# Mixture-of-experts stage: pairs of experts in two 64-column tiles replaced by quads in four 32-column tiles with wide passes of 128 slots

## Chip, cores and metric

One core of a Trainium2 chip runs the whole program: two transformer blocks over 512 tokens of width 1024, in fp32. The metric is the device time of one execution in microseconds (us), of which the median of several runs is given. The change touches one stage only, the hierarchical mixture of experts (MoE) of the first block.

## What is computed

The stage is this part of the reference, with 512 tokens, 4 groups of 8 experts, the best group and its two best experts for each token, and an expert width of 256:

```python
def hierarchical_moe(h, w_group, b_group, w_router, b_router, w_gate, w_up, w_down):
    t = h.reshape(-1, d)
    group_prob = jax.nn.softmax((t @ w_group + b_group), axis=-1)
    p_group, g_idx = lax.top_k(group_prob, 1)
    expert_logits = (t @ w_router + b_router).reshape(-1, N_GROUPS, EXPERTS_PER_GROUP)
    in_group = jnp.einsum('tg,tge->te', one_hot(g_idx[:, 0]), expert_logits)
    w_top, e_idx = lax.top_k(jax.nn.softmax(in_group, axis=-1), TOP_K)
    w_top = w_top / jnp.sum(w_top, axis=-1, keepdims=True) * p_group
    expert_ids = g_idx * EXPERTS_PER_GROUP + e_idx
    combine = jnp.sum(one_hot(expert_ids, N_EXPERTS) * w_top[..., None], axis=1)
    for e in range(N_EXPERTS):
        hid = jax.nn.silu(t @ w_gate[e]) * (t @ w_up[e])
        out = out + combine[:, e:e + 1] * (hid @ w_down[e])
    return out
...
    x = x + gate2[:, None, :] * ffn
```

Both kernels compute an expert only for the tokens that chose it. How many these are is known only during the run, so the number of passes is decided by branches.

## The kernel before

`Net.moe` begins by writing the normalised tokens to device memory (`h2d`) and working out, with comparisons and two matmuls, the `rank` of each token within each expert. An expert's tokens are then taken in slots: `select` (L1170 to L1178) compares ranks with a row of slot numbers (`iota`), and four small matmuls (L1174) turn the one-hot matrix into token numbers, weights and output rows. `gather` (L1193) fetches the tokens of the slots from `h2d` by an indirect DMA.

The 32 experts go through in 16 pairs, in the order of the list `order`. A pair is two neighbours of one group; each has 64 slots, and the two stand side by side in two 64-column tiles of the TensorE array. For a pair:

- `xpose` (L1214) transposes the gathered tokens by eight matmuls with the identity, and `feed` (L1202 on ScalarE, L1204 on VectorE) scales them into the tiles `xgT`.
- `expert1` (L1245) runs the gate and up projections: 8 slices of the depth, each for both experts, with 512 columns of weights; tanh (L1250) and two VectorE operations (L1251, L1252) make the hidden tile `mth`.
- `turn` (L1258) transposes the hidden tile by two matmuls, with an eviction on ScalarE (L1260).
- `expert2` (L1279) runs the down projection, ScalarE scales it by the weights (L1280), and GpSimd scatters the rows to `yd` by an indirect DMA (L1284). The last two pairs are added by matmuls instead (`combine`, L1293).

The loop over `n` places the gate/up of pair n ahead of the down of pair n - 1, so that the hidden tile of a pair is made and turned beside other matmuls.

When an expert of the pair has more than 64 tokens, `more` (L1318) runs a further pass of 64 slots, and a second one above 128 (L1324). `ahead` (L1305, L1307) gathers their tokens one pair early. The further passes are called through `again`; their tiles are `oxg`, `cy`, `th` and `rsb`. Passes beyond the third are all in `rest`, under one branch (L1379) that is taken when any expert has over 192 tokens. `count` (L1301) loads the larger count of a pair into a register of every engine.

The weights of an expert come in three tiles of 1 MiB, two for gate/up and one for down (`load`, L1026), all issued by SyncE from a pool of 12 tiles, which is two pairs. `load(n + 2)` stands behind the branches of pair n. At the end `fetch` (L1337) reads `yd` back in four transfers, each with both rows of 128 tokens; `collect` adds them on GpSimd (L1343), transposes them (L1347) and adds them to the residual (L1351).

A scheduler sets the order of each engine's instructions, and it may move one past a whole branch.

Of the kernel before, what the change touches and what calls it, by code (L numbers as in the profile page):

```python
# [46 lines left out]
def layout(a):  # L47
# [35 lines left out]
    gu = gu.reshape(NE, KT, P, 512).transpose(0, 2, 1, 3).reshape(NE, P, 4096)  # L83
# [45 lines left out]
def constants():  # L129
# [37 lines left out]
    o["iota"] = np.ascontiguousarray(np.broadcast_to(1 + np.arange(512).reshape(8, 64), (P, 8, 64)).astype(f))  # L167
# [36 lines left out]
class Net:  # L204
# [804 lines left out]
    def moe(self):  # L1009
        nc, v, s, g_, pe = self.nc, self.nc.vector, self.nc.scalar, self.nc.gpsimd, self.nc.tensor  # L1010
        A, tc, mp = self.A, self.tc, self.mp
        mm, ident, ones, mod = pe.matmul, self.ident, self.ones, self.mod

        wt = {}

        order = [4 * g + i for i in range(4) for g in range(4)]
        NP = NE // 2

        NL = 2

        def load(n, part=(0, 1)):

            for o in (0, 2048) * (0 in part) + (4096,) * (1 in part):
                for e in (2 * order[n], 2 * order[n] + 1):
                    w = wt[e, o] = self.t(self.mw, [P, 2048], "wmoe")
                    nc.sync.dma_start(w, A["wmoe"][e, :, o:o + 2048])  # L1026

        u128 = self.const("u128", [P, P], pool=mp)
        iota = self.const("iota", [P, 8, 64], pool=mp)
        tokens = iota.rearrange("p a b -> p (a b)")  # L1030
        prio = self.const("prio", [P, 8], pool=mp)
        tokb = self.const("tokb", [P, 4], pool=mp)
        load(0, (0,))
        load(1, (0,))
# [4 lines left out]
        xgs = [self.t(mp, [P, D], f"xg{q}") for q in range(3)]  # L1039
        oxg = [self.t(mp, [P, D], f"oxg{q}") for q in range(4)]  # L1040
        for t in xgs + oxg:
            g_.memset(t, 0.0)
# [3 lines left out]
        xn = [self.t(mp, [P, D], "htok", bufs=4) for _ in range(4)]  # L1046
        for i in range(4):
# [5 lines left out]
            nc.sync.dma_start(h2d[i * P:(i + 1) * P, :], xn[i])  # L1053
        load(0, (1,))
        load(1, (1,))
# [53 lines left out]
        cnt = sm([1, NE], "cnt")  # L1109
        v.tensor_copy(cnt, psr[0:1, 4, :])  # L1110
        cm = sm([1, 17], "cm")
        v.tensor_max(cm[:, 0:16], cnt[:, 0::2], cnt[:, 1::2])
        v.tensor_reduce(cm[:, 16:17], cm[:, 0:16], axis=AX.X, op=ALU.max)
        cmi = self.t(mp, [1, 17], "r_cmi32", I32)
        v.tensor_copy(cmi, cm)
# [22 lines left out]
        val = sm([P, 4, NP, 5], "val")  # L1138
# [11 lines left out]
        def oindex(p, r):  # L1150

            t = opair[p if r == 1 else NP + p % 4 if r == 2 else NP + 4]
            return (t if p >= NP - NL else t.bitcast(U32))[:, 0:1], t.bitcast(U32)[:, 1:2]

# [741 lines left out]
```

## Time and profile before

| what | value |
| --- | --- |
| median of 3 runs | 2215.34 us (2214.61 to 2220.91) |
| the profiled execution | 2215.8 us |
| its span, first to last instruction | 2214.0 us |
| TensorE (PE) busy, whole span | 2072.9 us, 94% |
| instructions, whole span | 32214 |
| MoE stage: its first weights issued | 447.55 us |
| first gate/up matmul | 493.41 us |
| last product into the residual ends | 855.32 us |
| weight tiles of the stage | 96 of 1024 KB, 11.7 us from issue to landing |

The span lies 1.8 us below the time of the same execution, and that time 0.5 us above the median. The share of TensorE over the whole span hides the stage: the blocks around it keep the engine busy all the time, while inside it the share changes from stretch to stretch. So the stage is read by stretches of its own, and then pair by pair. In the trace's names PE is the matmul engine, PEld its weight loads, DVE is VectorE, ACT ScalarE, POOL GpSimd and SP SyncE; a name with q behind it (PEldq) is the engine's instruction queue, where branches and register loads stand. One fp32 matmul of the code stands as two records.

### The profile page before, as it was taken

To read this page: it belongs to the slowest core of one execution; us is meant where nothing else is said; L and a number is where in the kernel's file an instruction comes from. 1 tells how busy PE (TensorE), PEld (TensorE's weight loads), DVE (VectorE), ACT (ScalarE), POOL (GpSimd) and SP (SyncE) were. 2 spreads that over 40 slices of the span, in tenths; PEclk is the share of its full clock that TensorE was granted. 3 is DMA by queue.
4 is the path that set the end of the run, shared out by engine and by line. 5 is a ranking of instruction groups with operands and counts; after the bars stand their busy time and mean duration, and the time that the engine had idled before them with its cause. 6 is when DMAs were issued, how large, how long until landed. Compare 5 with 4: busy or idle time off the path is not lost. (4 is left out here: it accounts for less than half of the span.)

```text
span 2214.0 us, 32214 instructions
## 1 busy us (share of the span) xinstructions
PE 2072.9 (94%) x12908; PEld 1569.1 (71%) x12908; DVE 1075.8 (49%) x2071; ACT 718.0 (32%) x1197; POOL 203.4 (9%) x223
## 2 busy tenths in 40 slices
PE   5999999788888978999999899999999999999996
PEld 3677767553433427888888888888878888888886
DVE  4663665642222217653253855746574447542444
ACT  3432442121222223322232434525352244322221
POOL 3020002010111113000001400000000032000002
PEclk9999999798898988999999999999999999999998
DMA  7343215075958972323332322323132322233321
GB/s 263 115 128 112 96 43 178 25 289 208 375 202 346 377 297 100 108 96 92 103 95 86 96 67 93 98 76 115 53 104 96 110 86 77 95 87 103 102 89 39
DMA packets 93877, 294.53 MB, mean 133 GB/s; under 512 B 15746, under 2 KB 27010, under 8 KB 81404
## 3 DMA queue, kind: packets, MB, share of 16 engines
q1 hardware_dynamic: 86364, 278.03, 36.2%
q0 software_dynamic: 7328, 14.01, 1.9%
q8 instruction: 119, 1.95, 0.3%
q14 instruction: 66, 0.54, 0.1%
HBM read 286.12 MB, written 20.23 MB: 138 GB/s over the span
## 5 line engine op out<-in xcount | busy, mean ns | idle before, releaser
L272 PE MATMUL mm<-xh,wh 128*128 128x512 f32 (+1 forms) x1584 | 614.4, 390 | 8.3 <-ACT xh L1510 4.5
L273 PE MATMUL mm<-xl,wh 128*128 128x512 f32 (+1 forms) x1584 | 604.7, 382 | 4.4 <-DVE xl L1511 4.2
L274 PE MATMUL mm<-xh,wl 128*128 128x512 f32 (+1 forms) x1584 | 602.1, 381 | 0.0
L255 ACT ACTIVATE wh<-wraw 128x1024 fp32r<-128x1024 f32 (+3 forms) x282 | 274.2, 974 | 745.7 <-PE mm L273 659.2
L256 DVE TENSOR_TENSOR wl<-wraw,wh 128x1024 fp32r<-128x1024 f32 (+3 forms) x282 | 315.0, 1118 | 192.9 <-ACT wh L255 187.4
L272 PEld LDWEIGHTS mm<-xh,wh 128*128 128x128 f32 x1584 | 301.4, 191 | 74.1 <-issue 8.0
L273 PEld LDWEIGHTS mm<-xl,wh 128*128 128x128 f32 x1584 | 302.4, 191 | 60.7 <-DVE xl L1511 6.2
L274 PEld LDWEIGHTS mm<-xh,wl 128*128 128x128 f32 x1584 | 301.6, 191 | 56.3 <-issue 1.2
L338 POOL TENSOR_TENSOR ss<-ss,sq 128x256 f32<-128x256 f32 (+1 forms) x69 | 67.0, 972 | 929.3 <-ACT sq L337 913.3
L272 PE MATMUL mm<-hh,wh 128*128 128x512 f32 (+1 forms) x416 | 148.5, 357 | 0.0
L274 PE MATMUL mm<-hh,wl 128*128 128x512 f32 (+1 forms) x416 | 148.3, 357 | 0.0
L273 PE MATMUL mm<-hl,wh 128*128 128x512 f32 (+1 forms) x416 | 148.3, 356 | 0.0
L1245 PE MATMUL mm<-wmoe,xgT 128*64 128x512 f32 x512 | 127.6, 655 | 5.9 <-issue 5.8
L1245 PEld LDWEIGHTS mm<-wmoe,xgT 128*64 128x64 f32 x512 | 41.4, 153 | 82.6 <-issue 74.7
L273 PEld LDWEIGHTS mm<-hl,wh 128*128 128x128 f32 x416 | 78.6, 189 | 11.4
L272 PEld LDWEIGHTS mm<-hh,wh 128*128 128x128 f32 x416 | 78.6, 189 | 11.2
L274 PEld LDWEIGHTS mm<-hh,wl 128*128 128x128 f32 x416 | 78.6, 189 | 11.2
L1571 DVE TENSOR_TENSOR sq<-mm,rsb 128x512 f32<-128x512 f32 x44 | 30.4, 691 | 104.0 <-PE mm L274 103.8
L1566 DVE TENSOR_TENSOR cy<-mm,rsb 128x512 f32<-128x512 f32 x44 | 30.4, 690 | 85.5 <-PE mm L274 83.5
L1251 DVE SCALAR_TENSOR_TENSOR mth<-mth,mm 128x256 f32<-128x256 f32 x16 | 6.7, 421 | 113.9 <-ACT mth L1250 113.9
L1279 PE MATMUL mm<-wmoe,hT 128*64 128x512 f32 x256 | 57.8, 592 | 0.0
L1202 ACT ACTIVATE xgT<-mm,mod,gs 128x128 f32<-128x128 f32 x64 | 27.9, 462 | 77.2 <-DVE xgT L1204 64.8
(495 smaller groups left out, 2620.6 us busy)
## 6 DMA issues: line engine op xcount, KB each, us to landing
wmoe<-in_wmoe SPq DMA_DIRECT2D x96, 1024.0 KB, 11.7
wraw<-in_win SPq DMA_DIRECT2D x90, 512.0 KB, 3.5
wraw<-in_wgu SPq DMA_DIRECT2D x88, 512.0 KB, 3.3
wraw<-in_wada SPq DMA_DIRECT2D x32, 512.0 KB, 3.7
wraw<-in_wd SPq DMA_DIRECT2D x32, 448.0 KB, 3.3
big<-in_wada SPq DMA_DIRECT2D x16, 512.0 KB, 6.0
wraw<-in_wd SPq DMA_DIRECT2D x16, 512.0 KB, 3.5
wraw<-in_wout SPq DMA_DIRECT2D x16, 256.0 KB, 2.5
```

The source lines that it names most:

```text
L255: self.nc.scalar.activation(h[:, :n], raw[:, :n], AF.Copy)
L256: self.nc.vector.tensor_sub(l[:, :n], raw[:, :n], h[:, :n])
L272: mm(ps, w1, xh[k], start=start and i == 0, stop=False)
L273: mm(ps, w1, xl[k], start=False, stop=False)
L274: mm(ps, w2, xh[k], start=False, stop=stop and i == nk - 1)
L338: self.nc.gpsimd.tensor_add(acc[:, hs], acc[:, hs], sq[:, hs])
L1202: s.activation(xTs[hf][:, k, :], pt[:, k, :], AF.Identity, scale=self.gs2[:, kk:kk + 1], bias=mod[:, 3, kk:kk + 1])
L1245: mm(pg_[cs, :], xT[k // 4][:, k % 4, cs], piece(p, c, k // 4 * 2048 + k % 4 * S, r), start=k == 0, stop=k == KT - 1)
L1251: v.scalar_tensor_tensor(th, th, 1.0, pg_[:, :256], op0=ALU.add, op1=ALU.mult)
L1279: mm(py[cs, :], hT[:, k, cs], piece(p, c, 4096 + k * 1024 + n * S, r), start=k == 0, stop=k == 1)
L1566: v.tensor_mul(t1, pp[0], rb)
L1571: v.tensor_mul(t2, pp[1], rb)
```

## The change

- Quads: the loop runs over 8 quads. Quad q holds expert q of each of the four groups, each with 32 slots, in four 32-column tiles.
- Wide passes: an expert's tokens beyond the first 32 go through `wide_pass`, with 128 slots of this expert alone on the whole array; up to four such passes are nested in `more`. Gate and up columns are stored in two halves (in `layout`), so that the first half's hidden tile is made beside the second half's matmuls. `gather_wide` gathers for a wide pass, and `ahead` does so for the first pass of each expert, behind the previous quad's passes.
- `rest` and its branch are gone. Down follows gate/up and turn of the same quad; it no longer stands behind the next one's gate/up.
- Weights come in six tiles of 512 KB for an expert, from a pool of 31. `load(31)` stands at the stage's start, and `load(6)` behind the passes of each expert.
- `count` loads six values for each quad (four experts, and the larger of each two), 48 in place of 17.
- The stores of `h2d` go from SyncE's queue to ScalarE's; only the last quad is added by matmuls, in place of two pairs.

The core of the diff (the added `layout` line for the halves, `select`, which does four experts with 32 slots, and the tail are left out):

```diff
+        NQ = NE // 4
+        first, wide = 32, 128
+        def ex(q, c):
+            return 8 * c + q
+        todo = iter([(ex(q, c), j) for q in range(NQ) for js in (range(4), range(4, 6)) for c in range(4) for j in js])
+        def load(n):
+            for e, j in islice(todo, n):
+                w = wt[e, j] = self.t(self.mw, [P, 1024], "wmoe")
+                nc.sync.dma_start(w, A["wmoe"][e, :, 1024 * j:1024 * j + 1024])
+        load(self.nmw)
...
-            nc.sync.dma_start(h2d[i * P:(i + 1) * P, :], xn[i])
+            nc.scalar.dma_start(h2d[i * P:(i + 1) * P, :], xn[i])
...
+        def gather_wide(e, r):
+            lo = first + wide * (r - 1)
+            v.tensor_tensor(oh1, iota[:, lo:lo + wide].unsqueeze(1).to_broadcast([P, 4, wide]),
+                            rank[:, :, e].unsqueeze(2).to_broadcast([P, 4, wide]), ALU.is_equal)
+            pv = self.pst([P, 3], "mm")
+            for i in range(4):
+                mm(pv, oh1[:, i, :], val[:, i, e, :], start=i == 0, stop=i == 3)
...
+            fetch_tokens(oxg[e // 8], u[:, 1:2])
...
+        def expert1(q, xT):
+            ps = self.pst([P, 2, 2, P], "mm")
             for k in range(KT):
+                for c in range(4):
+                    cs = slice(32 * c, 32 * c + 32)
+                    mm(ps[cs].rearrange("p a b c -> p (a b c)"), xT[k // 4][:, k % 4, cs], piece(ex(q, c), k),
+                       start=k == 0, stop=k == KT - 1, tile_position=(0, 32 * c))
+            th = self.t(mp, [P, 2, P], "mth")
+            glu(th, ps[:, :, 0, :], ps[:, :, 1, :])
             return th
...
+        def wide_pass(e, r):
+            xT = xpose(oxg[e // 8], oxT)
+            pt = None
+            for a in range(2):
+                ps = self.pst([P, 2, P], "mm")
+                for k in range(KT):
+                    mm(ps.rearrange("p a b -> p (a b)"), xT[k // 4][:, k % 4, :], piece(e, k)[:, 256 * a:256 * a + 256],
+                       start=k == 0, stop=k == KT - 1)
+                    if a and k == 4:
+                        pt = self.pst([P, P], "mm")
+                        pe.transpose(pt, oth[:, 0, :], ident)
+                        s.copy(ohT[:, 0, :], pt)
+                glu(oth[:, a, :], ps[:, 0, :], ps[:, 1, :])
+            py = [self.pst([P, S], "mm") for _ in range(2)]
+            for k in range(2):
+                if k:
+                    pt = self.pst([P, P], "mm")
+                    pe.transpose(pt, oth[:, 1, :], ident)
+                    s.copy(ohT[:, 1, :], pt)
+                for n in range(2):
+                    mm(py[n], ohT[:, k, :], wt[e, 4 + k][:, n * S:(n + 1) * S], start=k == 0, stop=k == 1)
+            for n in range(2):
+                s.activation(yt[1][:, n * S:(n + 1) * S], py[n], AF.Copy, scale=oix[e, r][:, 2:3])
+            scatter(yt[1], oix[e, r].bitcast(U32)[:, 0:1])
...
+        def ahead(q):
+            for h in range(2):
+                with tc.If(rvs[NE + 8 * h + q] > first):
+                    for c in (2 * h, 2 * h + 1):
+                        with tc.If(rvs[ex(q, c)] > first):
+                            gather_wide(ex(q, c), 1)
+        def more(e, r=1):
+            if r < 5:
+                with tc.If(rvs[e] > first + wide * (r - 1)):
+                    if r > 1:
+                        gather_wide(e, r)
+                    wide_pass(e, r)
+                    more(e, r + 1)
...
+        for q in range(NQ):
+            last = q == NQ - 1
+            th = expert1(q, xt)
+            if q == 0:
+                ahead(0)
+            if not last:
+                xt = xpose(gat[q + 1][0])
+                count(q + 1)
             hT = turn(th)
+            if not last:
+                expert2(q, hT, *gat[q][1:3])
+                if q + 2 < NQ:
+                    gat[q + 2] = gather(q + 2)
+            for c in range(4):
+                more(ex(q, c))
+                load(6)
+            if not last:
+                ahead(q + 1)
+        got = [fetch(i) for i in range(4)]
...
-                self.mw = pool(s1, "mw", 12, reuse_waits="tile")
+                self.nmw = 31
+                self.mw = pool(s1, "mw", self.nmw, reuse_waits="tile")
```

Three places of the program, as its engines receive it. `mm` is an accumulator, `wmoe` a weight tile, `c_ident` the identity, `xg` gathered tokens, `htok` in the changed kernel those of a wide pass, `cy` and `th` (in two tiles) the fed tokens and the hidden tile of a further or wide pass, `rsb` its turned hidden tile, `r_cmi` the counts, `r_val` and `cy` as operands of a small matmul the values and the one-hot matrix.

On TensorE before, where pair 2 follows pair 1, the turn of the pair before stands just ahead of the gate/up matmuls of the pair:

```order
L1214 MATMUL mm_5571<-c_ident_64,xg_725_4670 128x128 x4
L1214 MATMUL mm_5580<-c_ident_64,xg_725_4670 128x128 x4
L1258 MATMUL mm_5589<-c_ident_64,mth_5350 128x128 x2
L1245 MATMUL mm_5594<-wmoe_5296,xgT_899_5569 64x512
L1245 MATMUL mm_5594<-wmoe_5298,xgT_899_5569 64x512
```

On TensorE now, at the end of the first quad's gate/up:

```order
L1255 MATMUL mm_5114<-wmoe_4673,xgT_849_4956 32x512
L1227 MATMUL mm_5207<-c_ident_64,xg_4714 128x128 x4
L1227 MATMUL mm_5216<-c_ident_64,xg_4714 128x128 x4
L1264 MATMUL mm_5309<-c_ident_64,mth_5147 128x128 x2
L1287 MATMUL mm_5314<-wmoe_4675,hT_5312 32x512
```

The turn now belongs to the same quad: it follows its last gate/up matmul with only the eight transposes for the next quad between, and down follows at once.

On TensorE before, behind a further pass, from the end of its branches to the next pair:

```order
L1324 UNCONDITIONAL_BRANCH x2
L1318 UNCONDITIONAL_BRANCH
L1301 TENSOR_LOAD r_cmi_773_4820
L1305 COMPARE_AND_BRANCH
L1174 MATMUL mm_5766<-r_val_4849,cy_4854 128x5 x4
L1307 COMPARE_AND_BRANCH
L1174 MATMUL mm_5784<-r_val_4849,cy_4854 128x5 x4
L1307 UNCONDITIONAL_BRANCH x2
L1305 UNCONDITIONAL_BRANCH x2
L1174 MATMUL mm_5814<-r_val_4849,oh_5809 128x5 x4
```

On TensorE now, the end of an expert's first wide pass, and what is jumped over behind it when there is no second one:

```order
L1316 MATMUL mm_5414<-wmoe_4675,rsb_4926 128x512
L1316 MATMUL mm_5415<-wmoe_4675,rsb_4926 128x512
L1313 MATMUL mm_5418<-c_ident_64,th_4881 128x128
L1316 MATMUL mm_5414<-wmoe_4677,rsb_4926 128x512
L1316 MATMUL mm_5415<-wmoe_4677,rsb_4926 128x512
L1346 COMPARE_AND_BRANCH
L1202 MATMUL mm_5430<-r_val_4874,cy_4878 128x3 x4
L1227 MATMUL mm_5441<-c_ident_64,htok_751_4731 128x128 x4
```

Each expert has four such passes in its place in the code, one inside the other, where a pair had two.

On SyncE before, the loads of a pair stand between the branches of the look-ahead and those of the next pair's passes:

```order
L1305 COMPARE_AND_BRANCH
L1307 COMPARE_AND_BRANCH
L1307 UNCONDITIONAL_BRANCH x2
L1305 UNCONDITIONAL_BRANCH x2
L1026 DMA wmoe_5797<-in_wmoe 128x2048
L1026 DMA wmoe_5799<-in_wmoe 128x2048
L1026 DMA wmoe_5801<-in_wmoe 128x2048
L1026 DMA wmoe_5803<-in_wmoe 128x2048
L1026 DMA wmoe_5805<-in_wmoe 128x2048
L1318 COMPARE_AND_BRANCH
```

On SyncE now, behind the 31 loads of the start, the end of the 48 register loads and the first quad's passes:

```order
L1333 TENSOR_LOAD r_cmi_785_4845
L1333 ISA x2
L1346 COMPARE_AND_BRANCH x4
L1346 UNCONDITIONAL_BRANCH x5
L1031 DMA wmoe_5644<-in_wmoe 128x1024
L1346 COMPARE_AND_BRANCH x4
L1346 UNCONDITIONAL_BRANCH x5
```

All 48 register loads have moved ahead of the 32nd weight load, and that load alone stands behind the first expert's passes; the next 21 follow the branches of the other three experts and of the look-ahead.

## Rows read from the trace of the kernel before

**Rows 1.** Windows: stretch, length; busy us (count) by engine; PEclk; DMA share; GB/s

```profile
493.00:560.00 67.00, 56.21 (x257) 24.64 (x258) 19.58 (x81) 13.46 (x30) 10.51 (x9) 0.86 0.54 201
...
720.00:808.00 88.00, 79.68 (x373) 32.39 (x371) 18.67 (x61) 21.78 (x48) 10.12 (x10) 0.93 0.86 349
```

**Rows 2.** TensorE groups, 490 to 860 us: busy us, mean ns | idle before

```profile
L1245 PE MATMUL mm<-wmoe,xgT 128*64 128x512 f32 x512 | 127.6, 655 | 5.9 <-issue 5.8
L1279 PE MATMUL mm<-wmoe,hT 128*64 128x512 f32 x256 | 57.8, 592 | 0.0
...
L1245 PE MATMUL mm<-wmoe,cy 128*64 128x512 f32 x80 | 18.3, 599 | 0.3
```

**Rows 3.** TensorE timeline: start us, us, operation, count [idle before <-releaser]

```profile
493.41 7.09 PE L1245 MATMUL mm<-wmoe,xgT 128*64 128x512 f32 x32
...
522.68 1.09 PE L1214 MATMUL mm<-c_ident,oxg 128*128 128x128 f32 x8
523.84 3.65 PE L1245 MATMUL mm<-wmoe,cy 128*64 128x512 f32 x16
527.32 3.60 PE L1245 MATMUL mm<-wmoe,th 128*64 128x512 f32 x16
532.41 0.41 PE L1258 MATMUL mm<-c_ident,th 128*128 128x128 f32 x2 [1.48 <-DVEq L1324]
533.33 5.35 PE L1279 MATMUL mm<-wmoe,rsb 128*64 128x512 f32 x16 [0.52 <-ACT rsb L1260]
540.16 1.03 PE L1174 MATMUL mm<-r_val,oh 128*128 128x5 f32 x8 [1.48 <-PEq L1305]
...
543.32 7.65 PE L1245 MATMUL mm<-wmoe,xgT 128*64 128x512 f32 x32
550.81 3.60 PE L1279 MATMUL mm<-wmoe,hT 128*64 128x512 f32 x16
555.58 1.03 PE L1174 MATMUL mm<-r_val,oh 128*128 128x5 f32 x8 [1.17 <-PEq L1305]
```

**Rows 4.** Timeline, stage's end: reads of rows, an addition, last products

```profile
819.54 2.85 SPq L1337 DMA_DIRECT2D wmoe<-yd  x4
...
824.96 2.35 POOL L1343 TENSOR_TENSOR wmoe<-wmoe 128x1024 f32<-128x1024 f32 x1 [15.23 <-DMA wmoe<-yd]
...
851.10 4.22 DVE L1351 SCALAR_TENSOR_TENSOR x<-mm,mod,x 128x128 f32<-128x128 f32 x16
```

**Rows 5.** TensorE timeline at the only 32-column tiles of this kernel

```profile
129.40 0.64 PE L392 MATMUL sm<-wraw,ca 128*32 128x256 f32 x8
129.97 0.70 PE L636 MATMUL mm<-xx,c_ublk 128*128 128x512 f32 x1
```

**Rows 6.** Control by line: duration ns min/median/max, first and last start us

```profile
L1301 SPq TENSOR_LOAD <-r_cmi x16: 263/270/468, 481.4 to 779.8; - x16
...
L1301 PEldq TENSOR_LOAD <-r_cmi x16: 298/302/498, 497.8 to 795.0; - x16
...
L1318 PEldq COMPARE_BRANCH  x16: 70/348/922, 498.4 to 825.7; - x16
...
L1305 PEldq COMPARE_BRANCH  x19: 70/208/1011, 502.1 to 795.4; - x19
...
L1379 PEldq COMPARE_BRANCH  x1: 6410/6410/6410, 809.0 to 809.0; - x1
```

**Rows 7.** TensorE timeline behind the branch at L1379

```profile
817.66 0.66 PE L1258 MATMUL mm<-c_ident,mth 128*128 128x128 f32 x2 [7.98 <-DVEq L1379]
```

**Rows 8.** Windows as in the first group: two stretches of transfers

```profile
575.00:600.00 25.00, 22.02 (x85) 9.63 (x85) 6.93 (x29) 5.54 (x13) 5.10 (x5) 0.73 0.98 392
0.00:15.00 15.00, 0.00 (x0) 0.00 (x0) 4.74 (x9) 5.40 (x9) 7.04 (x13) 1.00 0.69 222
```

**Rows 9.** DMA issues of the page: count, KB each, us to landing

```profile
wraw<-in_wgu SPq DMA_DIRECT2D x88, 512.0 KB, 3.3
```

**Rows 10.** DMA queues of the page: packets, MB, share

```profile
q8 instruction: 119, 1.95, 0.3%
```

More of the change, by code (lines that the diff above doesn't have):

```diff
@@ L1 @@
 import math
-from itertools import chain
+from itertools import chain, islice
 import numpy as np
@@ new lines, in moe @@
+        v.tensor_copy(val[:, :, :, 0], tokb.unsqueeze(2).to_broadcast([P, 4, NE]))
+        v.tensor_copy(val[:, :, :, 1], wa)
+        v.scalar_tensor_tensor(val[:, :, :, 2], a2, float(S), tokb.unsqueeze(2).to_broadcast([P, 4, NE]), op0=ALU.mult, op1=ALU.add)
+        q1, q2, q3, q4 = (self.t(self.tp, [P, S], "cy" if q < 2 else "th") for q in range(4))
+        oix = {(e, 1): self.t(mp, [P, 4], f"oix{e}") for e in range(NE)}
+        for r in range(2, 5):
+            for c in range(4):
+                t = self.t(mp, [P, 4], f"oix_{c}_{r}")
+                oix.update({(ex(q, c), r): t for q in range(NQ)})
@@ L1270, in expert2 @@
+        def expert2(q, hT, idx, wv):
+            late = q == NQ - 1
+            ys = yt[:1]
             if late:
-                ys.append(oC if r else self.t(self.tp, [P, S], "sq", F32R))
+                ys = [self.t(mp, [P, D], f"ys{i}", F32R) for i in range(2)]
+                ys.append(self.t(self.tp, [P, S], "sq", F32R))
                 v.tensor_scalar(ys[-1], tokens, idx, None, op0=ALU.is_equal)
@@ L1294, in combine @@
                 v.scalar_tensor_tensor(self.x[k][:, hs], ps, mod[:, 5, k:k + 1], self.x[k][:, hs], op0=ALU.mult, op1=ALU.add)
-                yield
         rvs = {}
-        full = slice(0, S)
-        def count(p):
-            rvs[p] = nc.values_load(cmi[0:1, order[p]:order[p] + 1], min_val=0, max_val=S)
-        def ahead(p):
-            with tc.If(rvs[p] > 64):
-                gather(p, 1)
-                with tc.If(rvs[p] > 128):
-                    gather(p, 2)
-        def again(p, r, xg):
-            th = expert1(p, xpose(xg, r), r)
-            ys = expert2(p, turn(th, r), oindex(p, r)[0], oweight(p, r), r)
-            if p >= NP - NL:
-                drain(combine(ys, full))
@@ new lines, in ahead @@
+        def ahead(q):
+            for h in range(2):
+                with tc.If(rvs[NE + 8 * h + q] > first):
[9 more added lines that the diff above has]
+                    more(e, r + 1)
@@ L1344, in collect @@
+        def fetch(i):
+            ys = [self.t(self.mw, [P, D], "wmoe") for _ in range(2)]
+            for a in range(2):
+                nc.sync.dma_start(ys[a], yd[a * S + i * P:a * S + (i + 1) * P, :])
+            return ys
+        def collect(i, ys):
+            y = ys[0]
+            g_.tensor_add(y, y, ys[1])
             for hf in range(2):
```

225 lines of the change are left out of this document (71 added, 154 removed).

## The prediction

> **What bounds the kernel now.** I read the stretches of the stage first, then the costliest groups, then one pair's timeline, and last the control flow and the transfers. From 493 to 560 us TensorE is busy for 56.2 of 67 us, with a DMA share of 0.54; from 720 to 808 for 79.7 of 88, with 0.86 [rows 1]. So TensorE sets the end, and the transfers wait for it. Nearly all its time is two groups, the gate/up matmuls (127.6 us in the plain passes) and the down matmuls (57.8 us) [rows 2]. The reader is to see there that a matmul moves 512 columns, whether 2 or 60 of its 64 slots hold tokens.
>
> A plain pair costs 15.4 us, from the selection at 540.16 to that at 555.58; its parts are 8 transposes, the turn, 7.65 us of gate/up (7.09 where the clock was full) and 3.60 us of down. A further pass costs 17.5 us, from its transposes at 522.68 to the next selection at 540.16, since nothing covers it: between its gate/up and its down lie 2.41 us (from 530.92 to 533.33), its down takes 5.35 instead of 3.60 us after that gap, and another 1.48 us pass before TensorE works again [rows 3]. The gate/up of the further passes has 80 records of its first half, 16 a pass [rows 2], so there are five; the inputs say so too (expert loads of group 1: 117, 34, 64, 145, 73, 55, 84, 86; no expert of another group has over 29). So 16 pairs at about 15 us and 5 passes at 17.5 us make some 330 us of the way from 493.4 us, when gate/up begins, to the last addition's end at 855.3 [rows 3, 4].
>
> **What the change does to it, part by part.** On these inputs each quad has one expert over 32 tokens, of group 1, and never over 160: eight plain quads and eight wide passes, one in each quad.
>
> *Quads.* 32 gate/up matmuls on four 32-column tiles. What says that four run at once is the one place of the kernel with such tiles: eight records of 256 columns last 0.64 us, and the next instruction starts 0.57 us after the first [rows 5]. A pair's 32 records of 512 columns last 7.09 us, two at a time; by the same pace eight records of 256 would take 0.89 us two at a time and 0.44 four at a time, so 0.57 fits four with its start. A quad's gate/up then costs 7.0 us and its down 3.6, what a pair cost. The chain in the quad is now serial: gate/up 7.0, transposes for the next quad 1.09 (inside the gap), wait and turn up to 2.41 in all, down 3.6, selection 1.0, a branch and its drain 0.6. With the transposes counted whole, 15.7 us. I take 15.6, since a part of the gap covers them.
>
> *Wide pass.* Transposes and feed 1.16 us (522.68 to 523.84), 16 matmuls of 256 columns on the whole array, 32 records. A 512-column record alone takes 0.427 us (7.09/32 is 0.222 for one of two side by side, so twice that less the start), a 256-column one 0.213; 32 of these 6.8. Then 0.26 for a transpose in their midst, the wait of 2.41 behind the last of them (in part under the first two down matmuls of 1.7 us, which I count in it), and two more down matmuls 1.7: 12.4 us, against the 17.5 us of a 64-slot pass [rows 3]. Eight of them are 99 us, where five passes of before were 87.5. So here the change costs 12 us, while the plain part falls from 16 times 15.4 to 8 times 15.6, by 122 us.
>
> *Control between quads.* After the wide pass TensorE's queue passes two more experts' branches, six register loads at 0.302 us (1.8), and some six branches of the look-ahead at 0.208 median (1.2) [rows 6]. With 0.35 for each of three branches of the passes (1.0), the selection matmuls 1.0 and 0.9 for the one-hot ahead of them (an estimate: the gap of 1.48 less a load and two branches), 5.9 us. All of it is exposed; nothing is queued behind it that could run first. It comes seven times, and 4.9 once at the start. I add 0.6 for a drain and 2.0 a quad for the clock after gaps (5.35 against 3.60 [rows 3]; the granted clock of the two stretches is 0.86 and 0.93 [rows 1]).
>
> *What goes.* The big branch over all the fourth and later passes takes 6.41 us, and TensorE idles 7.98 [rows 6, 7]; that code is now inside each `more`, below.
>
> *Loads.* 192 half-MiB tiles. At 392 GB/s, the rate of a stretch with a share of 0.98, a quad's 24 tiles take 32.1 us; at the rate that the start of the kernel implies for short rows, 222 GB/s at a share of 0.69, so 322, they take 39.1 [rows 8]. I take 32, as that row is this very transfer. 18 of a quad's tiles come free only when its wide pass ends. At that point 13 of the next quad's 24 are in. A tile of this size lands 3.3 us after its issue where nothing queues [rows 9], about 2 more than its 1.34 of transfer, so the last three gate/up tiles are in 6 us later, under the 5.9 us of control and the first matmuls, and all eleven after 16.7, where down begins 0.6 + 5.9 + 7.0 + 1.09 + 2.41 = 17.0 us after. That is hidden, but without slack. The 48 register loads of SP, all ahead of its first wait for a free tile, take 48 x 0.27 = 13 us plus the check of their bounds [rows 6] and lie under the 31 tiles already issued (41 us at 392 GB/s).
>
> *Tail.* From the last wide pass: scatter and landing 6 us, the first read of the rows 3 to 5 (read issued 819.54, first addition 824.96), four additions of 2.35, last products 4.22: 22.6 us [rows 4]. The last quad's down and products run below it.
>
> *Sum.* 493.4 + 4.9 + 8 x (15.6 + 12.4 + 0.6 + 2.0) + 7 x 5.9 = 784.5; with the tail 807.1, against 855.3: 48.2 us less. The profiled execution took 2215.8 us, beside a median of 2215.3, so 2167.5 with no stall of code.
>
> **The unknown: code that is jumped over.** A `more` not taken now jumps over four nested wide passes, some 450 TensorE instructions (a matmul is four instructions, two weight loads and two records, as 512 records for 256 matmuls show, a transpose two; 20 matmuls and ten transposes a level make 100, four levels 400, and the gathers 48). Before, it jumped over two passes, some 230. Those branches took a median of 0.348 and at most 0.922 us; the only long one, over more than 10,000, took 6.41 [rows 6]. A quad jumps four times: once ahead of its wide pass, and three times in a row behind it, together about 1300 instructions. The trace has nothing between 230 and 10,000. The bounds of one quad's stall are 0 (each jump like those of before) and 16 us (two exposed stalls of 7.98, one ahead of the wide pass, one behind). A gain is excluded, since a jump that costs less than 0.35 us has been counted at that already. I take 1.4 us, near the short branches, as 450 is nearer to 230 than to 10,000; that makes 11 us and the forecast 2179. The instruction queue moves 119 blocks of 16 KB in the whole execution [rows 10], so code does arrive in blocks during the run.
>
> The Trainium skill ("Runtime: NRT & Kernel Launch", Instruction fetch mechanics) says that a taken branch whose target is outside the two blocks held must fetch the target's block before going on, with blocks of 256 instructions. The long jump of 6.41 us agrees; the short ones of 0.35 us agree in that their 230 instructions are inside one or two blocks. By that rule a jump of 450 could go either way, and the run of three behind the wide pass would stall; the time would be that of rival one or two below.
>
> **Rivals.** *One: one stall a quad*, at the run of three jumps behind the wide pass, which is five to six times what a jump of before skipped. Its price is the branch of 6.41 to the idle of 7.98 us [rows 6, 7], and as little as 4 if the queue runs ahead of TensorE by part of it: 2167.5 + 8 x 4 to 8 x 7.98 = 2200 to 2231, at 6.41 2219. Against it: the wide pass gives 12 us in which blocks may arrive. The break-even point is 48.2/8 = 6.0 us a quad.
>
> *Two, the one on the slow side: a stall at both places*, ahead of the wide pass and behind it, 12.8 to 16.0 us a quad: 2270 to 2295. It decides from two far jumps a quad on. For it: the jump ahead of the wide pass also skips twice the code of before, and the blocks arrive beside tiles at a share near 0.9. Against it: before, with a share of 0.86 in the last stretch [rows 1], no short branch took over 0.922.
>
> *Three: tiles bind.* At 39.1 us a quad against 36.5 the excess is 2.6 x 8 = 21 us: 2188 without stalls. The Trainium skill ("DMA: Bandwidth & Descriptors", Rules for kernel authors) wants 1 MiB or more in a transfer for the highest rate, which speaks against halving the tiles; no row here shows a half-MiB tile of this layout at a full share, so the 322 GB/s above stands as the bound.
>
> *Four: the change doesn't do what it says*: only two 32-column tiles run at once. Then gate/up and down cost 10.6 us more a quad, 85 in all: 2252. The 0.57 us of [rows 5] speaks against it.
>
> **How the numbers follow.** Forecast (stall of 0 to 3.5 us a quad): 2167 to 2195, 2179 likeliest, chance 0.47. One stall: 2200 to 2231, 0.25. Two stalls: 2270 to 2295, 0.20. Tiles: 2188, 0.05. Two tiles at once: 2252, 0.03. A measurement of this kernel tells 0.3%, 6.6 us, from no change: 2208.7 to 2222.0 is the same. Of one stall I give 0.04 to faster, 0.08 to the same and 0.13 to slower. So faster 0.47 + 0.05 + 0.04 = 0.56, the same 0.08, slower 0.13 + 0.20 + 0.03 = 0.36. The range goes from 2155 (clock losses of 2.0 a quad mostly absent, -12) to 2275, which leaves out most of two stalls and a little below, not over 0.2 in all. The likeliest case's own range is 2155 to 2195.
>
> **What would show it.** In the profile after: gate/up of a quad at about 7 us for 64 records (13 to 14 would be rival four); a wide pass of 12 to 13 us from transposes to its last down matmul; the last addition ending near 807 to 835; branches of `more` on TensorE's queue at or below 1 us (if some take 4 to 8 us, rival one or two, by how many in a quad); the idle before the next quad's first matmul put down to those branches, not to tiles (rival three: put down to the loads, with a share above 0.95). The prediction is wrong if any of the four jumps a quad costs over 6 us of TensorE's time, or if a quad's chain from gate/up to the next takes over 42 us.

## The result, and the profile after

The changed kernel takes 2351.11 us (median of 4 runs, 2346.82 to 2353.89), beside 2217.44 us for the kernel before in the same job. The ratio is 1.060 (95% interval 1.0576 to 1.0625): 6% slower, where 1.6% faster was forecast. The loss is 134 us between the medians, and it lies in the changed stage: the last product into the residual ends at 993.7 us in the profiled execution, against 855.3 before [rows 4], which is 138 us later, and the two profiled executions differ by 138 us too (2353.89 and 2215.8).

First the stretches, as in [rows 1]. Columns: start, end and length; busy us (count) of TensorE, its weight loads, VectorE, ScalarE, GpSimd; granted clock; DMA share; GB/s.

```profile
493.00:560.00 67.00, 29.76 (x238) 18.19 (x242) 14.60 (x80) 5.10 (x12) 2.16 (x2) 0.65 0.40 154
...
720.00:808.00 88.00, 57.25 (x360) 27.51 (x352) 13.54 (x46) 16.23 (x36) 7.09 (x7) 0.85 0.63 229
```

TensorE fell from 56.2 to 29.8 of 67 us and from 79.7 to 57.3 of 88, and the transfers fell too, from a share of 0.86 to 0.63 in the later stretch. Neither of them sets the end any more, so it must be waits. The list of what TensorE waited for from 490 to 1000 us (total, times, longest) names two:

```profile
PE mm L1202 <- DVE cy L1198: 120.1, 8, 21.2
PE sm L1108 <- DVE r_pre L1106: 46.0, 1, 46.0
```

The second comes once, at the start. The timeline there (start, duration, operation, count, idle time before and what ended it):

```profile
468.48 38.29 SPq L1031 DMA_DIRECT2D wmoe<-in_wmoe  x31
...
510.28 0.33 SPq L244 DMA_DIRECT2D c_prio<-in_prio  x1
...
517.82 0.17 DVE L1071 TENSOR_TENSOR r_gc<-r_gc,c_prio 128x16 f32<-128x16 f32 x1 [37.70 <-DMA c_prio<-in_prio]
...
538.67 1.02 PE L1255 MATMUL mm<-wmoe,xgT 128*32 128x512 f32 x2
```

Four small constants, among them the priorities `prio` that the routing multiplies with, stand on SyncE's queue behind the 31 weight tiles. Issuing those takes 38.3 us. VectorE stops in the middle of the routing for 37.7 us, and gate/up begins at 538.7 instead of 493.4 us [rows 3].

The first wait comes once a quad. The timeline of TensorE from the first quad's down to the second quad's gate/up:

```profile
555.86 5.34 PE L1287 MATMUL mm<-wmoe,hT 128*32 128x512 f32 x32 [1.63 <-ACT hT L1266]
561.01 0.45 PE L1172 MATMUL mm<-r_val,oh 128*32 128x3 f32 x32
565.66 1.94 PE L1227 MATMUL mm<-c_ident,htok 128*128 128x128 f32 x8 [4.19 <-PEq L1346]
...
578.38 1.98 PE L1316 MATMUL mm<-wmoe,rsb 128*128 128x512 f32 x4 [0.41 <-ACT rsb L1314]
601.57 1.84 PE L1202 MATMUL mm<-r_val,cy 128*128 128x3 f32 x8 [21.21 <-DVE cy L1198]
...
607.57 7.29 PE L1255 MATMUL mm<-wmoe,xgT 128*32 128x512 f32 x60
```

After the wide pass TensorE idles for 21.2 us. The row puts it down to VectorE's one-hot matrix, but VectorE takes 0.7 us for that and was itself waiting for TensorE's queue, whose matmuls read the same tile earlier (VectorE's own list has 135.1 us in 7 waits for L1340 on that queue). What the queue did is in the view by line, beside [rows 6] (ns, least, median, most):

```profile
L1346 PEldq COMPARE_BRANCH  x48: 82/3442/7442, 561.2 to 966.7; - x48
L1340 PEldq COMPARE_BRANCH  x24: 70/184/4670, 540.3 to 930.4; - x24
```

The branches of `more` went from a median of 0.348 and a most of 0.922 us to a median of 3.4 and a most of 7.4. Between 578 and 601 us three of them take 3.3, 5.9 and 6.1 us, and one of the look-ahead 4.7. Over the stage the 48 branches add up to 140 us (the sum of their durations). Only TensorE's queue is slow at them: the other engines pass the same branches in at most 0.063 us each.

### The profile page after: what moved, and what is told of

It is laid out like the page before. It is cut to its first block, busy times and chain, and to the rows that moved or that the text cites. A ratio compares the mean times of both kernels' runs of the same rounds, so it can differ in the third digit from the quotient of the medians.

```text
span 2352.1 us, 33140 instructions
## 1 busy us (share of the span) xinstructions
PE 2040.0 (87%) x13074; PEld 1571.8 (67%) x13074; DVE 1043.7 (44%) x1946; ACT 704.3 (30%) x1173; POOL 185.4 (8%) x208
## 4 chain that ended last, share of the span: by engine, by line
PE 52%; DVE 4%; POOL 1%; issue 1%; ACT 1%; DMA 0%; POOLq 0%; ACTq 0%; DVEq 0%
PE mm L274 16%; PE mm L275 16%; PE mm L273 16%; DVE xl L1520 1%; PE sm L1618 1%; POOL x L1472 1%; PE mm L1646 1%; POOL ss L339 0%; DVE wl L257 0%; DVE cy L1471 0%; PE mm L1643 0%; PE sm L1772 0%; PE sm L1633 0%; DVE rs_a L297 0%; PE mm L1287 0%
## 5 line engine op out<-in xcount | busy, mean ns | idle before, releaser
L1202 PE MATMUL mm<-r_val,cy 128*128 128x3 f32 x64 | 14.1, 340 | 122.6 <-DVE cy L1198 120.1
L1202 PEld LDWEIGHTS mm<-r_val,cy 128*128 128x128 f32 x64 | 13.5, 310 | 129.1 <-issue 129.1
L1255 PE MATMUL mm<-wmoe,xgT 128*32 128x512 f32 x512 | 81.1, 641 | 9.6 <-PEq L1338 5.2
L1215 ACT ACTIVATE xgT<-mm,mod,gs 128x128 f32<-128x128 f32 x32 | 14.6, 458 | 194.7 <-DVE xgT L1217 193.8
L1198 DVE TENSOR_TENSOR cy<-c_iota,r_rank 128x512 f32<-128x512 f32 x8 | 5.5, 692 | 136.2 <-PEq L1340 135.1
```

The source lines that it names most:

```text
L1202: mm(pv, oh1[:, i, :], val[:, i, e, :], start=i == 0, stop=i == 3)
L1255: mm(ps[cs].rearrange("p a b c -> p (a b c)"), xT[k // 4][:, k % 4, cs], piece(ex(q, c), k), start=k == 0, stop=k == KT - 1, tile_position ...
```

## Experiments: the start, and the code that is jumped over

The theory after the result had two parts: the constants cost some 45 us, and the jumps some 120. Its rivals: transfers are late anyway; a branch costs by being there or by being nested, not by what it skips; code waits behind weight tiles. Single runs are set against 2351.11 us, the median of the changed kernel.

**Constants first.** Line moved:

```diff
-        load(self.nmw)
         u128 = self.const("u128", [P, P], pool=mp)
...
         tokb = self.const("tokb", [P, 4], pool=mp)
+        load(self.nmw)
```

> Edit: the four constants of the stage are loaded ahead of the first 31 weight tiles instead of behind them; nothing else. In the changed kernel VectorE waits 37.7 us for the constant prio, which stands on SyncE's queue behind 31 tiles. Theory (the constants are late, and nothing else is at the start): first gate/up moves from 538.7 us to about 497 to 502, the time falls by 37 to 42 us, to 2310 to 2315. Rival (the 31 tiles are the limit themselves, constants or not, because the tokens or the first weights land behind them): the wait moves to another transfer and the time falls by less than 20 us, to above 2332.

Measured: 2305.46 us, 45.7 less. The constants are issued from 453 us and the tiles from 471, VectorE's wait is gone, and gate/up begins at 500.7 us, as its timeline shows:

```profile
454.13 0.43 SPq L244 DMA_DIRECT2D c_prio<-in_prio  x1
...
471.00 40.78 SPq L1031 DMA_DIRECT2D wmoe<-in_wmoe  x31
...
500.71 0.59 PE L1255 MATMUL mm<-wmoe,xgT 128*32 128x512 f32 x1
```

The gain is a little over the expected 37 to 42: 38.0 us of it is the earlier start, and the other 7.7, later in the stage, are about what the four runs of the changed kernel differ by (7.1). The rival falls: 31 tiles ahead of the tokens did not hold gate/up up.

**One level of wide pass.**

```diff
-            if r < 5:
+            if r < 2:
                 with tc.If(rvs[e] > first + wide * (r - 1)):
```

> Edit: only the first wide pass of an expert is left in the code; the second to fourth, nested in it, none of which runs on these inputs, are left out. The number of branches not taken stays at three a quad for the experts without a wide pass, but each jumps over about 100 TensorE instructions instead of about 450, and the one inside the wide pass is gone. Theory of distance (a jump costs by the code it skips): the branches of more fall from 3.3 to 7.4 us to under 1 us each, a quad falls from 55 to about 38 us, the time by 130 to 160 us to 2190 to 2222. Rival of structure (each branch not taken costs some microseconds whatever it skips): only the inner branch's 0.3 to 3.8 us a quad go, time above 2320. Rival of traffic (code waits behind weight tiles): branches stay at 3 us or more, since tiles flow as before.

Measured: 2235.18 us, 115.9 less, somewhat above the expected 2190 to 2222. The branches of `more`, and the first of TensorE's waits of before, in this kernel:

```profile
L1346 PEldq COMPARE_BRANCH  x40: 70/212/352, 562.1 to 851.6; - x40
...
PE mm L1202 <- DVE cy L1198: 24.4, 8, 3.3
```

No branch is over 0.352 us, though those of the next two experts are still there behind each wide pass and not taken. So a branch does not cost by being there, and weight tiles, which flow faster here than in the changed kernel (299 GB/s from 540 to 850 us, against 229), do not make it cost by themselves.

**Both.**

> Edit: both of the former at once, constants ahead of the tiles and one level of wide pass (the deeper ones, which don't run on these inputs, are left out). If the two causes are independent, the savings add: 2352 less about 40 less 130 to 160 is 2150 to 2182. If the two share a wait (with a quicker quad the tiles, 32 us a quad at 392 GB/s, end last), less than the sum: 2185 to 2210, with TensorE waiting for wmoe loads.

Measured: 2186.15 us. The savings of the two runs add up to 161.6, which would be 2189.5: as far as single runs tell, the two causes are independent. It is above the first expectation of 2150 to 2182 by what one level saved less than expected, and inside the second (2185 to 2210). But if the two causes shared a wait, the savings would come to less than their sum, and they come to 165.0; that tiles hold back the quads with one level shows further below. The branches' durations fall from 140.9 (constants first) to 8.8 us in sum, by 132, and the time by 119.3, so not all of their duration was a loss. A quad takes 40.5 us here (from wide pass to wide pass, 561.4, 602.0, 642.5).

**How far a jump may go**, on top of the constants first, by two and three levels in place of four, and then without nesting: four copies of the pass under one branch for the experts that have none on these inputs.

```diff
-                    wide_pass(e, r)
-                    more(e, r + 1)
+                    for _ in range(1 if e // 8 == 1 else 4):
+                        wide_pass(e, r)
```

> Edit, on top of the constants ahead of the tiles: two nested levels of wide pass in place of four (the third and fourth, which don't run on these inputs, are left out). A branch of more not taken jumps over 227 to 232 TensorE instructions, as the branches of the kernel before did, against 104 with one level (2186 us) and 475 with four (2305 us). Theory that a jump only costs when it passes what was already on its way: as with one level, branches under 1 us apart from the second and third of jumps in a row, 2186 to 2215. Rival (cost in proportion to the code skipped): (228 - 104)/(475 - 104) = a third of 119 us, so 2226.

> Edit, on top of the constants ahead of the tiles: three nested levels (the fourth, which doesn't run on these inputs, is left out). Jumps over 350 to 355 instructions. Theory of steps (a jump either finds its target or stalls for 3 to 7 us): the branches fall into two kinds, under 0.5 us and above 2.5 us, and at 352 some of the branches ahead of the wide pass are of the first kind, while those in a row behind it mostly stall; 2240 to 2290. Rival in proportion: two thirds of 119, 2265, with each branch at some 3 to 4 us and none short.

> Edit, on top of the constants ahead of the tiles: the experts of group 1, which have a wide pass on these inputs, have one level; those of the other groups, which have none, have four copies of the pass one behind another under a single branch, not nested (none of them runs; with other inputs the result would not be the reference's). 106 instructions to skip in group 1's place, 408 to 412 in the other three. Theory of distance: branches of the other groups at 3 to 7 us as with nested levels, time 2280 to 2305 less the branch inside the pass, so about 2275 to 2300. Rival (the nesting is what costs, not the distance): all branches under 1 us and 2186.

Measured: 2230.81, 2258.29 and 2251.31 us. The first total lies nearer to the rival in proportion (2226) than to the theory of steps (2186 to 2215), and the second fits both (2265, and 2240 to 2290). The branches one by one tell them apart. In each fence is first the second or third quad's branch ahead of the wide pass, with the entry and, where there is one, the inner branch; then the row of those behind the pass. With two levels, a jump of 230:

```profile
L1346 PEldq COMPARE_BRANCH  x3: 70/325/325, 560.2 to 575.3; - x3
...
L1346 PEldq COMPARE_BRANCH  x3: 184/1341/6017, 577.5 to 579.3; - x3
```

With three, a jump of 351:

```profile
L1346 PEldq COMPARE_BRANCH  x3: 70/325/345, 562.5 to 578.4; - x3
...
L1346 PEldq COMPARE_BRANCH  x3: 184/942/6871, 580.6 to 582.0; - x3
```

Not nested, 408 to 412:

```profile
L1346 PEldq COMPARE_BRANCH  x2: 82/1828/3573, 613.5 to 617.3; - x2
...
L1346 PEldq COMPARE_BRANCH  x3: 187/5230/5910, 628.6 to 634.9; - x3
```

A jump of 230 or 351 that stands alone takes 0.33 us, as one of 104 does; at three levels it does so in six of eight quads. At 408 to 412 it takes 1.4 to 3.8 us in all eight. But behind the wide pass, where the inner jump, and those of the next two experts follow one another, the second takes mostly some 1 us and the third 5 to 8 in all quads but one, at 230 already. So there are steps, and a row of jumps costs more than its parts alone: two jumps of 104 cost nothing (the run with both edits), an inner one of some 120 and two of 230 do. What counts in a row stays open. It is not simply the sum of what was passed: with three levels the second jump stands at a sum of some 600 (an inner one of 351 less 104, and 351) and mostly takes 1 us, while with two levels the third stands at some 590 and takes 5 to 6. Those second jumps are also of neither kind that was expected (under 0.5 and above 2.5 us). The third run shows that nesting is not needed: its branches add up to 101 us. It came out 24 us below its expectation; in two quads the first jump behind the pass took 0.4 us, and what else made it less was not tried.

**Without the tiles' traffic**, with the changed kernel's four levels: only the first quad's tiles are loaded, and all compute with them.

```diff
-            return wt[e, k // 2][:, k % 2 * S:k % 2 * S + S]
+            return wt[e // 8 * 8, k // 2][:, k % 2 * S:k % 2 * S + S]
...
-                load(6)
```

> Edit: four levels of code as in the changed kernel, but only the first quad's 24 weight tiles are loaded, and all quads compute with them (so the results of seven quads are not the reference's); no weight traffic after the first 33 us of the stage. Rival of traffic: the branches of more fall to about 1 us or less, a quad to about 38 us, time 2190 to 2230. Theory of distance: the branches stay at about 3 to 7 us and the time only loses the 7 tiles ahead of the constants (9 us) and some slowing of code fetches: 2315 to 2345. In between (branches at half): both, distance sets that code must be fetched and traffic how long it takes.

Measured: 2289.61 us, between the two. Of the 61.5 us, 12 are at the start (fewer tiles ahead of the constants; gate/up begins at 526.6 us).

```profile
L1346 PEldq COMPARE_BRANCH  x48: 70/2890/5167, 548.7 to 903.6; - x48
...
PE mm L1202 <- DVE cy L1198: 90.1, 8, 14.7
```

The branches fall from 140 to 106 us in sum, the most from 7.4 to 5.2. So the skipped code costs without the traffic too, and the traffic makes it dearer by a third. The tiles also lengthen TensorE's own work: in the first seven quads down takes 3.64 us here, and 5.3 to 7.4 in the changed kernel.

## Experiments: a version that keeps the gain, and what limits it

**The deeper passes at the end.** One level in the quads; the second to fourth pass of an expert in a block of its own under one branch, which loads the expert's tiles again. On these inputs the block does not run.

```diff
+        def rest():
+            top = nc.values_load(cmi[0:1, NE + 16:NE + 17], min_val=0, max_val=S)
+            with tc.If(top > first + wide):
+                for e in range(NE):
+                    with tc.If(rvs[e] > first + wide):
+                        for j in range(6):
+                            wt[e, j] = self.t(self.mw, [P, 1024], "wmoe")
+                            nc.sync.dma_start(wt[e, j], A["wmoe"][e, :, 1024 * j:1024 * j + 1024])
+                        deep(e, 2)
...
+        ys = expert2(NQ - 1, hT, *gat[NQ - 1][1:3])
+        rest()
         got = [fetch(i) for i in range(4)]
```

> Edit, on top of the constants ahead of the tiles: one level of wide pass in the quads, and the second to fourth in a block of their own behind the last quad, under one branch (as rest in the kernel before), which loads the expert's six tiles once more; the last quad's down goes ahead of that branch. With these inputs nothing in the block runs. Theory: 2186 of one level plus the jump over some 12000 instructions, 6 to 8 us if exposed, or nothing if the scatter and the read of the rows cover it: 2186 to 2195, faster than before by 1.0 to 1.3%. Rival (the far jump delays the engines that scatter and read back too): above 2197.

Measured: 2187.15 us (2182.54 to 2190.89), ratio to the kernel before 0.9877 (0.9845 to 0.9908). The total is 1.0 us above that of both edits, which says little, as that was a single run. The far jump is not free. Its branch, then the last scatter and the read of the rows behind it, in this run:

```profile
L1356 PEldq COMPARE_BRANCH  x1: 4110/4110/4110, 798.9 to 798.9; - x1
...
797.69 1.00 POOL L1271 DMA_INDIRECT yd<-ys,oix  x1 [22.78 <-ACTq L1347]
...
804.86 3.84 SPq L1376 DMA_DIRECT2D wmoe<-yd  x8
```

And the last two in the run with both edits, which has no such branch:

```profile
803.72 1.00 POOL L1270 DMA_INDIRECT yd<-ys,oix  x1 [22.37 <-ACTq L1346]
...
807.05 3.83 SPq L1356 DMA_DIRECT2D wmoe<-yd  x8
```

From the scatter to the read it is 7.2 us here (6.7 to 7.2 in all five runs that have the block) and 3.3 there, so the block with its jump delays the read by 3.8 us: the rival's mechanism, at a price too small for its total (above 2197). It is paid once, where the code in the quads cost 119.3. So this kernel, called g1 from here on, beats both others, by 1.2% and 7.0%.

**Two waits of TensorE taken away.** In g1 TensorE still waits 3.3 us a quad for the look-ahead's one-hot matrix, and passes two branches behind the wide pass. One run moves the look-ahead behind the quad's own gate/up, one puts one branch over the two, one does both.

```diff
-            if not last:
-                ahead(q + 1)
...
             hT = turn(th)
+            if q:
+                ahead(q)
```

```diff
-            for c in range(4):
+            for c in range(2):
                 more(ex(q, c))
                 load(6)
+            with tc.If(rvs[NE + 8 + q] > first):
+                for c in (2, 3):
+                    more(ex(q, c))
+            load(12)
```

> Edit, on top of g1: the look-ahead (counts and the gathering for the wide passes) of a quad stands behind its own gate/up and turn, no longer behind the wide pass of the quad before. Theory: TensorE's wait of 3.1 to 3.7 us for the one-hot matrix after each wide pass (26 us in all with one level) goes, since gate/up runs there, and the gathering lies beside the hidden tile's chain: 2187 less 15 to 25, so 2162 to 2172. Rival: the tokens now arrive too late (an indirect read takes some 8 us from issue to landing, and only down, the selection and a branch lie between), so the wide pass waits 3 us or more and the time stays within 2180 to 2195.

> Edit, on top of g1: the passes of the experts of groups 2 and 3 stand under one more branch on the larger of their counts, so that one jump over some 212 instructions takes the place of two over 104 in a row. Theory: each branch not taken behind the wide pass costs about 1.9 us even when its code is near (from branch to branch 572.4 to 574.3 in the run with one level), so 8 x 1.5 to 1.9 us go: 2187 less 12 to 15, so 2172 to 2175. Rival one (fixed cost is hidden or is paid by the new branch): 2183 to 2190. Rival two (212 at once stalls): above 2200.

> Edit: both of the former on top of g1. If they are independent: 2187 less 27 to 40, so 2147 to 2160. If the tiles then set the pace (24 tiles a quad take 32 us at 392 GB/s and 34.5 at the 365 seen with one level, against a quad of 40.6 us less 4 to 6): 2160 to 2175, with TensorE or its weight loads waiting for wmoe transfers.

Measured: 2190.40, 2186.55 and 2196.21 us, ratios to the kernel before 0.9885 (0.9869 to 0.9902), 0.9868 (0.9852 to 0.9885) and 0.9910 (0.9893 to 0.9926). None is faster than g1 by more than the runs scatter, and the one with both is slower: each of its runs (2193.58 to 2199.04) is above each of g1's. It lies above both of its expected ranges. The second lands in the range of its rival one, so a branch less brought nothing. The first lands in its rival's range but not for its reason, since TensorE waits for the late tokens once only:

```profile
PE mm L1203 <- DVE cy L1199: 19.3, 8, 3.7
...
PE mm L1228 <- DMA htok<-h2d,oix: 4.4, 1, 4.4
```

The wait for the one-hot matrix did not go: it is 26.1 us in g1 and 19.3 here, now behind gate/up. And down takes longer, 8.8 us in one quad (637.2 to 646.0) and 7.7 on average over six, against 6.3 in g1.

**Without the tiles' traffic, from g1.** So what sets the pace of g1's quads, at 38 to 41 us from wide pass to wide pass? The same edit as above, on g1.

> Edit, on top of g1: only the first quad's 24 weight tiles are loaded and all quads compute with them (so the results of seven quads are not the reference's). It asks why a quad with one level takes 41.1 us where the sum of the prediction has 36.5, and why taking TensorE's waits away (the two runs before) brought nothing. Theory that the tiles pace the quads (share 0.93, 363 GB/s in g1): without them a quad falls to 36 to 38 us and the time by 25 to 40 us, to 2147 to 2162. Rival (TensorE's own chain: gate/up 9.7 and down 5.6 us busy a quad in g1 against 7.0 and 3.6 in the prediction, from the clock after gaps and small matmuls between): a quad stays at 40 to 41 us and the time falls by less than 12 us, mostly at the start.

Measured: 2159.19 us, 28.0 less than g1. The timeline of g1, from a quad's gate/up to the next wide pass:

```profile
615.70 1.92 PE L1256 MATMUL mm<-wmoe,xgT 128*32 128x512 f32 x2
...
619.02 7.15 PE L1256 MATMUL mm<-wmoe,xgT 128*32 128x512 f32 x60
627.56 0.44 PE L1265 MATMUL mm<-c_ident,mth 128*128 128x128 f32 x2 [1.40 <-DVE mth L1249]
628.46 1.84 PE L1288 MATMUL mm<-wmoe,hT 128*32 128x512 f32 x9 [0.46 <-ACT hT L1267]
...
631.36 4.33 PE L1288 MATMUL mm<-wmoe,hT 128*32 128x512 f32 x19
636.33 1.06 PE L1228 MATMUL mm<-c_ident,htok 128*128 128x128 f32 x8 [0.64 <-PEq L1347]
```

And without reloads:

```profile
593.43 1.06 PE L1228 MATMUL mm<-c_ident,htok 128*128 128x128 f32 x8 [1.34 <-DVEq L1347]
...
611.28 8.67 PE L1256 MATMUL mm<-wmoe,xgT 128*32 128x512 f32 x64 [0.96 <-PEq L1339]
...
622.46 3.64 PE L1288 MATMUL mm<-wmoe,hT 128*32 128x512 f32 x32 [0.46 <-ACT hT L1267]
...
627.71 1.07 PE L1228 MATMUL mm<-c_ident,htok 128*128 128x128 f32 x8 [1.34 <-DVEq L1347]
```

This quad falls from 41.1 (595.2 to 636.3) to 34.3 us; over the first six steps from wide pass to wide pass the mean falls from 39.4 to 34.3, and the seventh, which has no down, stays at 30. The down of a quad is the clearest: 32 records in 3.64 us, four at a time, against 7.2 us. In g1 its first 12 records go three at a time, and of the fourth expert's, four stand at the very end and run alone, 0.43 us each, which is what a group of four takes together. That makes twelve rounds in place of eight, some 5.2 us. The rest of the 7.2 is TensorE's clock: behind the gaps around the turn (1.40 and 0.46 us idle) it falls to the lower level, with a granted clock of 0.50 from 630.0 to 632.5 us, and the records there take up to 1.06 us instead of 0.59. Over the six quads down takes 6.3 us on average, so it makes 2.7 of the 5.1 us a quad. The order is the scheduler's; without reloads, where no tile can come late, it does not arise. So the tiles set g1's pace, by their transfers and by the order that comes with them; how the 28 us divide between the two was not tried. The stretch from 560 to 640 us, in g1 and then without reloads:

```profile
560.00:640.00 80.00, 65.26 (x396) 30.55 (x395) 14.53 (x50) 16.21 (x36) 8.12 (x8) 0.91 0.93 363
```

```profile
560.00:640.00 80.00, 66.12 (x434) 37.14 (x434) 16.36 (x57) 19.34 (x45) 9.11 (x9) 0.94 0.11 34
```

The transfers are at 0.93 in g1, which leaves little to win for whoever only takes waits of TensorE away. What is left without the tiles, 34 GB/s or 1.2 MB in a quad's 34.3 us, is mostly the gathering and scattering of tokens.

## Why the prediction was wrong

The step that failed is the price of the code that is jumped over, 1.4 us a quad where the runs show 14.9; two smaller terms that were set at nothing, the start and the tiles, add to it. From 2351.1: 45.7 for the constants, 119.3 for the code (constants first against both), 28.0 for the tiles, with 1.0 back for the block at the end, leave 2159.2. The account closes by construction, each term being the difference of two kernels' times, and three of these times are of single runs. In the changed kernel a quad took 54.5 us on average from wide pass to wide pass, past the 42 that the text named as a sign of being wrong.

*The start* was taken over from the kernel before ("493.4"). Under loads the text followed the weight tiles and the 48 register loads on SyncE's queue, and did not ask what else had stood behind the first tiles: the four constants. The diff shows it, with `load(self.nmw)` above the lines of the constants where `load(0, (0,))` stood below them. 45.7 us.

*The code that is jumped over* was the unknown, between 0 and 16 us a quad, and 1.4 was taken, "as 450 is nearer to 230 than to 10,000". It is 14.9 us a quad (119.3/8), and 119.3 where the forecast has 11. The row that it leaned on, 0.35 us for 230 instructions, comes from branches that stand alone; the run with two levels shows that 230 is already too far for the third in a row. The text named the three jumps in a row, with about 1300 instructions, as the case for rival one, and then priced the forecast by the single jump. Rival two had the mechanism and the price, 12.8 to 16 us a quad, though not the places: it counted two stalls a quad, and the trace has three or four branches over 3 us in each. Its 2270 to 2295 plus the constants' 45.7 is 2316 to 2341; with an unknown whose upper bound is well past the break-even point of 6.0 us, 0.20 was little for it.

*The tiles* were "hidden, but without slack", at 32.1 us against a quad of 36.5. The sum of bytes left out the tokens: 1.2 MB a quad beside 12.6, at 392 GB/s 3.0 us more, so 35.1 (an estimate) against the 34.3 that TensorE needs. Since 18 tiles come free at once behind the wide pass, the queues may also have little to do ahead of it; that this, the order of down and the clock make up the rest of g1's 39.4 us a quad is argued, not tested. It is rival three's mechanism, by another quantity than half-MiB tiles, which moved 363 GB/s at a share of 0.93, little less for their share than the 1 MiB tiles before with 392 at 0.98 [rows 8]. The changed kernel has it too, as its down of 5.3 to 7.4 us shows.

*What held.* The sum without stalls was 2167.5, and the run without the skipped code and the tiles' traffic took 2159.2. That is in part luck. There, the way from the first gate/up to the end of the last wide pass took 270.7 us for 291.1; against that, gate/up began 7.6 us later (501.0 for 493.4), and the tail took 29.4 us for 22.6, of which 3.8 is the far jump and 2.8 the read of the rows up to the first addition (5.8 us, counted at 3, where [rows 4] have 5.4). Four 32-column tiles run at once: 60 records of 512 columns in 7.06 to 7.29 us. The wide pass takes 12.6 us (561.4 to 574.1 in the run with both edits) for 12.4. The control between quads takes 5.5 us there (574.1 to 579.6) for 5.9. The quad without tile traffic takes 34.3 us for 36.5, so of the 2.0 added for the clock little was needed there.

The Trainium skill ("Runtime: NRT & Kernel Launch", Instruction fetch mechanics) says that a taken branch to code outside the two blocks held waits until the target's block is fetched. The runs agree with it for jumps that stand alone, in that 351 instructions are free in six of eight quads and 408 to 475 are dear; where the borders of the blocks lay, no run shows. That several short jumps in a row do the same at 230 each is what the runs add.

## What to carry to other kernels

Code that does not run is not free: a branch over 408 to 475 TensorE instructions mostly took 3 to 7 us here, and the last of a row of shorter jumps did too. Keep what is skipped often short, and put what is rare under one branch at the end, where the far jump is paid once (3.8 us here). When a load is moved, go down its whole queue and ask for every transfer behind it who waits for that, down to constants of a few bytes. And where a bound of an unknown cost is past the break-even point, its case is not a small one.

## What was not expected of the hardware

- The same jump of 230 instructions took 0.33 us alone and 5 to 6 us as the last of a row (the run with two levels); a far one over some 12,000 took 4.1 us, less than many over 475.
- Without weight traffic the same jumps cost 106 instead of 140 us in sum.
- A 512-column record on one 32-column tile alone takes 0.43 us, and four on four tiles take 0.43 together, so an order that leaves out the fourth and does it later costs as much as a whole further round.
- Down, 3.6 us with four tiles side by side, took up to 7.2 us where the order left gaps and the granted clock fell to 0.50 in its midst.
